# Seven-product blocks in all four feed-forward stages, woven side work in the down projections, some low parts of weights by accumulating DMA

## The chip, the cores and the metric

The kernel runs on one core of a Trainium2 chip. The metric is the device time of one execution in microseconds, as the median of several runs.

## The reference, cut to what matters

The program is two network blocks after each other on a sequence of 512 tokens with 1024 features. The first has two layers, each a feed-forward stage, a token mixing (three kinds of attention) and another feed-forward stage. The second is a state-space and a gated linear recurrence, merged and projected, with a gated side input. The four feed-forward stages are what the change touches most:

```
def swiglu(h, w_gate, w_up, w_down):
    return (jax.nn.silu(h @ w_gate) * (h @ w_up)) @ w_down

for l in range(DEPTH):                                   # 2
    x = x + 0.5 * swiglu(rmsnorm(x, ffn1_norm[l]), ...)  # 1024 -> 2816 -> 1024
    x = x + token_mixing(rmsnorm(x, mix_norm[l]), ...)
    x = x + 0.5 * swiglu(rmsnorm(x, ffn2_norm[l]), ...)
x = rmsnorm(x, final_norm)
x = second_block(x, ...)
```

## The kernel before, in words

Activations lie with features on the partitions: eight tiles `xt[m]` of 128 x 512. Every product of two float32 matrices is made of three matmuls on rounded operands (`mm3`, lines 171 to 173): high part by high part, high part of the weights by the low part of the activations, low part of the weights by the high part of the activations. So each weight tile is split after it is loaded: `wload` (line 155) loads up to 1024 columns into one of three `raw` buffers on SP's queue, ScalarE copies each piece of 512 columns to the rounded high part `whi` (line 164), VectorE subtracts to get the low part `wlo` (line 165). There are four buffers for each of the two. `split` (line 175) does the same for activations and for the blocks' weight sums.

Four feed-forward stages run in the order 0 to 3, with a mixing after stages 0 and 2. Stages 0 and 3 go through `ffn` (line 227): in two halves, 11 row groups of gate and up products of 8 x 3 matmuls with 512 columns each, then the down projection over all eight output tiles. A `hook` is a generator with side work, one step of which is issued before each row group: `positions` (line 420) builds the attention biases for stage 0, `prepare` (line 1001) the tables and operands of the second block's recurrence for stage 3.

Stages 1 and 2 go through `ffn_blocks` (line 319). The first four row groups are plain; meanwhile `blocks` (line 330) combines halves of the activations. The other 18 row groups go in pairs through `gate_up` (line 275): each pair of row groups (`j` 0 for gate, 1 for up) is a 2 x 2 block product made with seven products in place of eight, by sums of weight blocks (`s1` to `s4`, made on VectorE at lines 284 to 287) and of activation blocks; each product is 4 x 3 matmuls with 256 columns. One such pass of seven products takes two raw buffers, and 14 pieces for the split weights, which `piece` (line 268) hands out in turn from the buffers of `whi` and `wlo` and twelve more. The activation tiles `xh`, `xl` are overwritten with the combined activations by 16 splits when the plain rows are done. After row groups 8, 16 and 22 a down projection of that group's rows follows and adds to `xt`.

`block2` (line 1158) is the second block. In its front half four generators (`s5`, `lru`, `merge_gates`, `first_norm`) are stepped in a fixed order of fractions; their projections load weights by `wload` as well, and POOL does some elementwise products (lines 1231, 1309, 1326).

All waits come from the tile framework. It also sets the order of the instructions in each engine's queue by a schedule that it makes at build time, with the program's order as priority; the engines then run their queues in order.

Of the kernel before, what the change touches and what calls it, by code (L numbers as in the profile page):

```python
# [17 lines left out]
P = 128  # L18
# [34 lines left out]
BLOCKS = (1, 2)  # L53
# [46 lines left out]
def body(tc, A, out, tap, upto=99):  # L100
# [7 lines left out]
    with ctx:  # L108
# [45 lines left out]

        def wload(src, n):
# [3 lines left out]
            for i in range(0, n, WP):  # L159
# [5 lines left out]
                weng[0].tensor_tensor(lo[:, :w], r, hi[:, :w].bitcast(F32), op=ALU.subtract)  # L165
# [61 lines left out]
        def ffn(i, nxt, pre, hook=None):  # L227
            with tc.tile_pool(name=f"fp{i}", bufs=1, reuse_waits="tile") as fp:
                for hf in range(2):
                    hh, hl = [], []  # L230
                    for f in range(NH):
                        ff = hf * NH + f
                        if hook is not None and ff >= 1:
                            if ff == 1:
                                work = hook(fp)
                            next(work, None)
                        gp = psum("pg")
                        up = psum("pu")
                        for j, o in ((0, gp), (1, up)):
                            wh, wl = ahead if i == ff == j == 0 else wload(A[f"gu{i}"][ff, :, j, :], KD * P)  # L240
                            for k in range(KD):
                                c = slice(k * P, (k + 1) * P)
                                mm3(o, wh[:, c], wl[:, c], xh[KORD[k]], xl[KORD[k]], k == 0, k == KD - 1)
                            if ff == 0:
                                next(pre)
                        t = tmp("t")
                        u = tmp("u")
                        V.tensor_tensor(t, gp, rstd, op=ALU.mult)
                        act(t, t, AF.Silu)
                        V.tensor_tensor(u, up, rstd, op=ALU.mult)  # L250
                        V.tensor_tensor(u, u, t, op=ALU.mult)
                        a = fp.tile([P, S], F32R, tag="h", name="hh", bufs=2 * NH)
                        b = fp.tile([P, S], F32R, tag="h", name="hl", bufs=2 * NH)
                        split(a, b, u)
                        hh.append(a)
                        hl.append(b)
                    for m in range(KD):
                        o = psum("pd")
                        for k0, k1 in ((0, 6), (6, NH)):
                            wh, wl = wload(A[f"dn{i}"][m][:, (hf * NH + k0) * P:(hf * NH + k1) * P], (k1 - k0) * P)  # L260
                            for k in range(k0, k1):
                                c = slice((k - k0) * P, (k - k0 + 1) * P)
                                mm3(o, wh[:, c], wl[:, c], hh[k], hl[k], k == 0, k == NH - 1)
                        V.scalar_tensor_tensor(out=xt[m], in0=o, scalar=0.5, in1=xt[m], op0=ALU.mult, op1=ALU.add)
                        if hf == 1 and nxt is not None:
                            nxt.tile(m)

# [7 lines left out]
        def gate_up(p, j, xk, fp, turn):  # L275
# [43 lines left out]
        def ffn_blocks(i, nxt, pre):  # L319
            with tc.tile_pool(name=f"fp{i}", bufs=1, reuse_waits="tile") as fp:  # L320
# [32 lines left out]
                for g, (f0, f1) in enumerate(FGRP):  # L353
# [8 lines left out]
                    for p in range(f0 // 2, f1 // 2):  # L362
                        if p < NCLS:
                            for f in (2 * p, 2 * p + 1):
                                t, u = None, None
                                for j in range(2):
# [22 lines left out]
                                    if f > 0 and len(ts) < KD:  # L389
                                        blocks(len(ts) // 2)  # L390
# [1236 lines left out]
```

## Time and profile before

| | us |
|---|---|
| median of 3 runs | 2675.55 (2673.48 to 2675.76) |
| the profiled execution | 2671.1 |
| its span, first to last instruction | 2669.3 |
| TensorE busy | 2563.2 (96%) |
| VectorE busy | 1852.2 (69%) |
| ScalarE busy | 1290.5 (48%) |
| GpSimd busy | 108.9 (4%) |

PE is TensorE's matmuls, PEld its weight loads, DVE VectorE, ACT ScalarE, POOL GpSimd, SP the engine that issues the loads. Busy time is a union of an engine's instructions; matmuls overlap, so the mean duration of one is longer than the distance from one start to the next. A stage's limit is read from a table of stretches: how much of the stretch each engine is busy, and who waits for whom in it.

### The profile page before, as it was taken

Reading aid. Unit: us, or ns where it says so; the run is one execution under the profiler, and the core shown is the slowest. Engines: PE = TensorE matmul, PEld = TensorE weight load, DVE = VectorE, ACT = ScalarE, POOL = GpSimd, SP = SyncE. Lnnn points to the kernel's source line nnn. Section 1 sums busy time; section 2 is a strip of 40 time slices with the busy share of each in tenths; the row PEclk is TensorE's granted clock in tenths of the full one; section 3 lists DMA queues with packets and bytes.
Section 4 is the critical chain, followed back from the end, with each engine's and each line's share of the span. In section 5 each row is a group of like instructions: output and inputs, shape, how many; then the busy total and the mean of one; then the engine's idle time right before and its main releaser. Section 6 shows DMA issues by size and latency. Waiting matters only on the chain.

```text
span 2669.3 us, 36064 instructions
## 1 busy us (share of the span) xinstructions
PE 2563.2 (96%) x13140; PEld 2132.9 (80%) x13140; DVE 1852.2 (69%) x3533; ACT 1290.5 (48%) x2382; POOL 108.9 (4%) x113
## 2 busy tenths in 40 slices
PE   8999999999999999899999999999999978889998
PEld 6888888777789998889888877788888767668885
DVE  8634457888777586867676888766464699994435
ACT  5423346656445454535355666543343454563342
POOL 0000000000000000000000000000000013210001
PEclk9999999999999999999999999999999989989998
DMA  7432245763233332232335575233342444323332
GB/s 236 135 102 95 89 148 176 223 200 91 96 103 103 95 105 93 79 104 95 111 107 186 172 237 146 93 134 124 124 152 84 154 143 140 123 75 123 102 107 91
DMA packets 124354, 340.12 MB, mean 127 GB/s; under 512 B 17296, under 2 KB 25488, under 8 KB 123664
## 3 DMA queue, kind: packets, MB, share of 16 engines
q1 hardware_dynamic: 124176, 337.82, 40.1%
q8 instruction: 103, 1.69, 0.3%
q14 instruction: 75, 0.61, 0.1%
HBM read 279.56 MB, written 51.90 MB: 124 GB/s over the span
## 4 chain that ended last, share of the span: by engine, by line
PE 79%; DVE 14%; DMA 3%; ACT 2%; issue 2%; POOL 0%; POOLq 0%; SPq 0%; DVEq 0%; ACTq 0%
PE pd L172 6%; PE pd L171 6%; PE pd L173 6%; PE pg L171 4%; PE pg L172 4%; PE pg L173 4%; PE pu L171 3%; PE pu L172 3%; PE pu L173 3%; PE s L554 2%; PE sy L171 2%; DMA raw<-in_gu 2%; PE sy L173 2%; PE sy L172 2%; PE tp L583 1%
## 5 line engine op out<-in xcount | busy, mean ns | idle before, releaser
L164 ACT ACTIVATE whi<-raw 128x512 fp32r<-128x512 f32 (+1 forms) x738 | 431.8, 590 | 782.0 <-PE pd L172 237.9
L165 DVE TENSOR_TENSOR wlo<-raw,whi 128x512 fp32r<-128x512 f32 (+1 forms) x738 | 475.1, 649 | 366.9 <-ACT whi L164 319.4
L172 PE MATMUL pd<-hl,whi 128*128 128x512 f32 x704 | 278.1, 395 | 0.0
L173 PE MATMUL pd<-hh,wlo 128*128 128x512 f32 x704 | 278.1, 395 | 0.0
L171 PE MATMUL pd<-hh,whi 128*128 128x512 f32 x704 | 278.0, 395 | 0.0
L171 PE MATMUL pg<-xh,whi 128*128 128x512 f32 x480 | 192.4, 401 | 7.7 <-ACT xh L211 7.7
L172 PE MATMUL pg<-xl,whi 128*128 128x512 f32 x480 | 191.0, 398 | 0.3 <-DVE xl L212 0.3
L173 PE MATMUL pg<-xh,wlo 128*128 128x512 f32 x480 | 190.6, 397 | 0.0
L173 PEld LDWEIGHTS pd<-hh,wlo 128*128 128x128 f32 x704 | 132.0, 187 | 32.2
L171 PEld LDWEIGHTS pd<-hh,whi 128*128 128x128 f32 x704 | 132.0, 187 | 32.1
L172 PEld LDWEIGHTS pd<-hl,whi 128*128 128x128 f32 x704 | 132.0, 187 | 32.0
L171 PE MATMUL pu<-xh,whi 128*128 128x512 f32 x384 | 152.3, 397 | 0.0
L172 PE MATMUL pu<-xl,whi 128*128 128x512 f32 x384 | 151.6, 395 | 0.0
L173 PE MATMUL pu<-xh,wlo 128*128 128x512 f32 x384 | 151.3, 394 | 0.0
L171 PE MATMUL sy<-xh,wsp 128*128 128x256 f32 x432 | 123.0, 285 | 5.4 <-ACT c L304 4.2
L176 ACT ACTIVATE wsp<-fs 128x512 fp32r<-128x512 f32 x144 | 88.1, 627 | 70.3 <-DVE fs L284 43.1
L172 PE MATMUL sy<-xl,wsp 128*128 128x256 f32 x432 | 121.2, 280 | 0.0
L173 PE MATMUL sy<-xh,wsp 128*128 128x256 f32 x432 | 121.1, 280 | 0.0
L171 PEld LDWEIGHTS pg<-xh,whi 128*128 128x128 f32 x480 | 90.9, 189 | 29.9 <-ACT xh L211 8.7
L172 PEld LDWEIGHTS pg<-xl,whi 128*128 128x128 f32 x480 | 90.7, 189 | 23.4 <-DVE xl L212 2.2
L173 PEld LDWEIGHTS pg<-xh,wlo 128*128 128x128 f32 x480 | 90.8, 189 | 22.3
L177 DVE TENSOR_TENSOR wsp<-fs,wsp 128x512 fp32r<-128x512 f32 x144 | 92.2, 685 | 6.0 <-ACT wsp L176 5.6
(629 smaller groups left out, 6471.4 us busy)
## 6 DMA issues: line engine op xcount, KB each, us to landing
raw<-in_gu SPq DMA_DIRECT2D x176, 512.0 KB, 3.6
raw<-in_w SPq DMA_DIRECT2D x44, 512.0 KB, 3.7
raw<-in_dn SPq DMA_DIRECT2D x48, 384.0 KB, 3.2
b<-bias SPq DMA_DIRECT2D x64, 256.0 KB, 4.0
raw<-in_dn SPq DMA_DIRECT2D x32, 512.0 KB, 3.6
raw<-in_wf SPq DMA_DIRECT2D x28, 512.0 KB, 4.4
raw<-in_dn SPq DMA_DIRECT2D x32, 320.0 KB, 2.9
raw<-in_wo SPq DMA_DIRECT2D x16, 512.0 KB, 3.7
```

The source lines that it names most:

```text
L164: act(hi[:, :w], r, AF.Copy)
L165: weng[0].tensor_tensor(lo[:, :w], r, hi[:, :w].bitcast(F32), op=ALU.subtract)
L171: nc.tensor.matmul(o, wh, ah, start=first, stop=False, skip_group_check=more)
L172: nc.tensor.matmul(o, wh, al, start=False, stop=False, skip_group_check=more)
L173: nc.tensor.matmul(o, wl, ah, start=False, stop=last, skip_group_check=more)
L176: act(dst_h, src, AF.Copy)
L177: eng.tensor_tensor(dst_l, src, dst_h.bitcast(F32), op=ALU.subtract)
L554: nc.tensor.matmul(sps, a[:, c], b, start=i == 0, stop=i == len(passes) - 1)
L583: nc.tensor.transpose(tp[:, k * P:(k + 1) * P], e[:, k * P:(k + 1) * P], ident)
```

## The change

All four stages go through one `ffn`, which is the old `ffn_blocks` with a hook. The hook's generator is stepped in the down projections, by a count for each of the three groups: 4, 4, 1 for `positions`, 7, 8, 4 for `prepare`. Its tiles come from a pool that is open during one down projection, and the blocks' extra pieces and sums from a pool that is open during one group of row pairs, so that both use the same memory. The passes' weights are made by `blocks_of`, apart from their products; for the first pass this stands ahead of the 16 activation splits.

`lowpart` makes a low part in one of two ways: by VectorE as before, or by a ScalarE copy with scale -1 into the low tile and a DMA from POOL's queue that adds the raw weights to it. The second way is used for `a12` and `a22` of every pass, for plain row groups 1 to 3 of every stage, and for all weights in the front half of `block2`.

```diff
-BLOCKS = (1, 2)
+LDMA = ("a12", "a22")
...
+        def lowpart(lo, r, hi, by_dma):
+            if by_dma:
+                act(lo, r, AF.Copy, scale=-1.0)
+                G.dma_start(out=lo.bitcast(F32), in_=r, accum_op=ALU.add)
+            else:
+                V.tensor_tensor(lo, r, hi.bitcast(F32), op=ALU.subtract)
...
-                weng[0].tensor_tensor(lo[:, :w], r, hi[:, :w].bitcast(F32), op=ALU.subtract)
+                lowpart(lo[:, :w], r, hi[:, :w], weng[0] is None)
...
-        def gate_up(p, j, xk, fp, turn):
+        def blocks_of(p, j, xk, fp, turn):
...
-                ws[n] = piece(fp, turn), piece(fp, turn)
-                split(*ws[n], w)
+                ws[n] = h, lo = piece(fp, turn), piece(fp, turn)
+                act(h, w, AF.Copy)
+                lowpart(lo, w, h, n in LDMA)
+            return ws
+
+        def gate_up(ws, xk):
...
-        def ffn_blocks(i, nxt, pre):
+        class Late:
+
+
+            def tile(self, *a, **k):
+                return self.pool.tile(*a, **k)
+
+        def ffn(i, nxt, pre, gain, hook=None, steps=(0, 0, 0)):
...
+                late = Late()
+                work = hook(late) if hook else iter(())
...
+                        weng[0] = V if f == 0 else None
+                        wh, wl = ahead if i == f == j == 0 else wload(W[f, :, j, :], KD * P)
+                        weng[0] = V
...
+                for f in range(2 * NCLS):
+                    rows(f)
                 for g, (f0, f1) in enumerate(FGRP):
...
+                    with tc.tile_pool(name=f"fw{i}{g}", bufs=1, reuse_waits="tile") as fw:
+                        turn = [0]
+                        for p in range(max(f0 // 2, NCLS), f1 // 2):
+                            ws = blocks_of(p, 0, xk, fw, turn)
+                            if p == NCLS:
                                 for m, t in enumerate(ts):
                                     split(xh[m], xl[m], t)
...
+                            row_pair(lambda: gate_up(ws, xk), lambda: gate_up(blocks_of(p, 1, xk, fw, turn), xk))
                     n = f1 - f0
...
+                    with tc.tile_pool(name=f"fq{i}{g}", bufs=1, reuse_waits="tile") as late.pool:
+                        done = 0
+                        for m in range(KD):
+                            o = psum("pd")
+                            wh, wl = wload(A[f"dn{i}"][m][:, f0 * P:f1 * P], n * P)
...
+                            while done < steps[g] * (m + 1) / KD:
+                                next(work, None)
+                                done += 1
                         if f1 == NF:
+                            for _ in work:
+                                pass
...
         def block2(pre):
+            weng[0] = None
...
+                weng[0] = V
                 with tc.tile_pool(name="bd", bufs=1, reuse_waits="tile") as bd:
...
-                    if 2 * l in BLOCKS:
-                        ffn_blocks(2 * l, nrm, (cur.done(), f"ffn1_norm{l}"))
-                    else:
-                        ffn(2 * l, nrm, cur.done(), positions if l == 0 else None)
+                    ffn(2 * l, nrm, cur.done(), f"ffn1_norm{l}", positions if l == 0 else None, (4, 4, 1))
...
+                    ffn(2 * l + 1, nrm, cur.done(), f"ffn2_norm{l}", prepare if l + 1 == DEPTH else None, (7, 8, 4))
```

In `positions` the tiles of the row positions are loaded and converted three times (`along`) in place of once, with twelve buffers in place of seven; in `prepare` there are five buffers in place of six and one table buffer in place of two, and `kk` is loaded for each quarter.

## Rows read from the trace of the kernel before

**Rows 1.** The page, part 1: busy us, share of the span, instructions.

```profile
PE 2563.2 (96%) x13140; PEld 2132.9 (80%) x13140; DVE 1852.2 (69%) x3533; ACT 1290.5 (48%) x2382; POOL 108.9 (4%) x113
```

**Rows 2.** Stretches: start:end length, busy us (count) per engine, clock, DMA.

```profile
core 0: us, PE busy (x) PEld busy (x) DVE busy (x) ACT busy (x) POOL busy (x), PEclk, DMA share, GB/s
...
684.50:1042.80 358.30, 351.85 (x2245) 317.77 (x2244) 262.39 (x458) 175.84 (x332) 1.01 (x1) 0.99 0.30 97
1042.80:1409.00 366.20, 354.65 (x2246) 318.44 (x2245) 262.42 (x458) 173.74 (x331) 1.01 (x1) 0.99 0.32 101
...
1710.60:2092.20 381.60, 381.60 (x1694) 308.98 (x1693) 230.72 (x543) 158.38 (x278) 5.25 (x13) 1.00 0.37 121
2092.20:2410.00 317.80, 275.88 (x1184) 215.78 (x1183) 284.64 (x467) 173.95 (x259) 64.20 (x66) 0.92 0.39 127
```

**Rows 3.** Stretches inside the stages, columns as in rows 2.

```profile
199.00:322.00 123.00, 123.00 (x529) 98.95 (x528) 56.42 (x87) 40.64 (x66) 0.00 (x0) 1.00 0.28 89
730.50:779.00 48.50, 42.31 (x338) 41.71 (x337) 42.06 (x74) 26.46 (x55) 0.00 (x0) 0.93 0.31 105
779.00:824.00 45.00, 45.00 (x196) 36.20 (x195) 22.82 (x36) 13.66 (x23) 0.00 (x0) 1.00 0.27 87
824.00:904.00 80.00, 79.77 (x671) 79.53 (x670) 65.63 (x120) 45.88 (x93) 0.00 (x0) 1.00 0.31 100
1089.00:1139.60 50.60, 43.07 (x338) 41.76 (x337) 42.15 (x74) 26.19 (x55) 0.00 (x0) 0.93 0.32 99
1184.40:1268.60 84.20, 81.27 (x674) 80.11 (x673) 66.01 (x120) 45.68 (x94) 0.00 (x0) 1.00 0.30 96
1710.60:1840.50 129.90, 129.90 (x590) 105.68 (x589) 98.13 (x284) 58.15 (x99) 4.05 (x7) 1.00 0.38 130
1902.10:2030.60 128.50, 128.50 (x578) 104.33 (x577) 75.19 (x145) 54.24 (x93) 1.20 (x6) 1.00 0.38 130
```

**Rows 4.** TensorE's waits, 730 to 779 us: who waited, us in total, times, longest.

```profile
PE sy L173 <- DVE wsp L177: 5.4, 1, 5.4
```

**Rows 5.** Chain that ended last, 1184 to 1270 us: start, us, what.

```profile
1211.86 4.23 DMA raw<-in_gu
...
1221.85 4.29 DMA raw<-in_gu
```

**Rows 6.** Timeline around 1216 us: start, us, instruction, idle time before and its releaser.

```profile
1216.18 0.69 DVE L284 TENSOR_TENSOR fs<-raw 128x512 f32<-128x512 f32 x1 [2.48 <-DMA raw<-in_gu]
...
1216.97 0.63 ACT L176 ACTIVATE wsp<-fs 128x512 fp32r<-128x512 f32 x1 [1.95 <-DVE fs L284]
1217.51 0.36 ACT L304 ACTIVATE c<-sy 128x256 f32<-128x256 f32 x1
```

**Rows 7.** TensorE's waits, 1184.4 to 1375 us, columns as in rows 4.

```profile
PE sy L171 <- ACT c L304: 3.7, 6, 1.4
```

**Rows 8.** Groups of instructions, 824 to 904 us: shapes, count, busy us, mean ns, idle.

```profile
L177 DVE TENSOR_TENSOR wsp<-raw,wsp 128x512 fp32r<-128x512 f32 x21 | 14.1, 685 | 1.5 <-ACT wsp L176 1.3
...
L176 ACT ACTIVATE wsp<-raw 128x512 fp32r<-128x512 f32 x21 | 13.0, 631 | 7.4 <-PE sy L172 5.6 <-ACT c L308 1.0 <-ACT wsp L176 0.5
```

**Rows 9.** DMA queues (packets, MB, share) and issues (KB each, us to landing).

```profile
q1 hardware_dynamic: 124176, 337.82, 40.1%
...
qka<-sta SPq DMA_DIRECT2D x16, 256.0 KB, 5.1
...
gd<-g SPq DMA_DIRECT2D x8, 256.0 KB, 2.0
```

**Rows 10.** Groups and waits of the last block's front half, 2130 to 2410 us.

```profile
L165 DVE TENSOR_TENSOR wlo<-raw,whi 128x512 fp32r<-128x512 f32 (+1 forms) x74 | 54.1, 747 | 4.9 <-ACT whi L164 4.7
...
PE yp L172 <- DVE hs L177: 10.7, 7, 2.3
PE yp L171 <- ACT hs L176: 10.7, 4, 5.7
...
L1326 POOL TENSOR_TENSOR g<-g,e 128x512 f32<-128x512 f32 x10 | 14.9, 1493 | 57.1 <-ACT e L1325 57.1
L1309 POOL TENSOR_TENSOR c<-c,ig 128x512 f32<-128x512 f32 x10 | 14.8, 1483 | 54.7 <-ACT ig L1307 54.6
```

More of the change, by code (lines that the diff above doesn't have):

```diff
@@ L225, in done @@
                 yield col
[L227 to L266, printed above, removed]
         def piece(fp, turn):
@@ new lines, in ffn, with finish, rows @@
+                hh, hl = [], []
+                def finish(u):
+                    a, b = htile("hh"), htile("hl")
+                    split(a, b, u)
+                    hh.append(a)
+                    hl.append(b)
+                def rows(f):
+                    o = [None, None]
+                    for j in range(2):
+                        o[j] = psum("pg")
+                        weng[0] = V if f == 0 else None
+                        wh, wl = ahead if i == f == j == 0 else wload(W[f, :, j, :], KD * P)
+                        weng[0] = V
+                        for k in range(KD):
+                            c = slice(k * P, (k + 1) * P)
+                            mm3(o[j], wh[:, c], wl[:, c], xh[KORD[k]], xl[KORD[k]], k == 0, k == KD - 1)
+                        if f == 0:
+                            next(pre)
+                        elif len(ts) < KD:
+                            blocks(len(ts) // 2)
+                    t, u = tmp("t"), tmp("u")
+                    V.tensor_tensor(t, o[0], rstd, op=ALU.mult)
+                    act(t, t, AF.Silu)
+                    V.tensor_tensor(u, o[1], rstd, op=ALU.mult)
+                    V.tensor_tensor(u, u, t, op=ALU.mult)
+                    finish(u)
@@ L437, in positions, with along @@
                 V.tensor_copy(lo, it)
+            def along():
+                pi, pt, rh, rl = tmp("pi", I32), tmp("pt", I32), tmp("rh"), tmp("rl")
+                dma(pi, A["posr"])
+                parts(pi, pt, rh, rl)
+                return rh, rl
+            parts(ci, ct, ch, cl)
             for q in range(4):
+                if q % 2 == 0:
+                    rh, rl = along()
                 d = tmp("d")
@@ L1002, in tmp @@
             def tmp(name):
[L1003 removed]
+                return fp.tile([P, S], F32, tag="pz", name=name, bufs=5)
             def softplus():
@@ L1087, in prepare @@
             for ct in range(4):
+                kk = fp.tile([P, 256], F32, tag="kk", name="kk")
+                dma(kk, A["kk"])
                 g4 = slice(4 * ct, 4 * ct + 4)
@@ L1530, in body @@
                     weng[0] = V
-                    if 2 * l + 1 in BLOCKS:
-                        ffn_blocks(2 * l + 1, nrm, (cur.done(), f"ffn2_norm{l}"))
-                    else:
-                        ffn(2 * l + 1, nrm, cur.done(), prepare if l + 1 == DEPTH else None)
+                    ffn(2 * l + 1, nrm, cur.done(), f"ffn2_norm{l}", prepare if l + 1 == DEPTH else None, (7, 8, 4))
                     for m in range(KD):
```

92 lines of the change are left out of this document (24 added, 68 removed).

## The prediction

> **What bounds the kernel now.** I began with the busy line of the page: TensorE is busy 2563 of 2669 us [rows 1]. VectorE, at 69%, bounds only where a stage makes it late. So two things can be sold: matmul columns, and the about 106 us in which TensorE has nothing to run. The stretches of the second view show where each lies [rows 2]. The fourth feed-forward stage, written as plain products like the first, has no idle time: 381.6 us busy of 381.6. The second and the third, already in seven-product blocks, take 358.3 and 366.2 us, 6.4 and 11.5 us of it idle. The front half of the last block (2092 to 2410) is different: VectorE is busy 284.6 of 317.8 us, TensorE 275.9, at a mean granted clock of 0.92.
>
> Then the parts of a stage [rows 3]. In plain rows 529 matmuls of 512 columns start in 123.0 us, 0.2325 us each. In blocks, where a matmul has 256 columns, 671 take 80.0 us in the second stage (0.119 us each, against a half of 0.2325, 0.116) and 674 take 84.2 us in the third (0.125). The first two block pairs of both stages are the weak place: 336 matmuls should take 39.1 us and take 48.5 and 50.6. The wait there is one: 5.4 us for the low part of the first weight piece [rows 4]. It sits on VectorE behind the 16 splits of the combined activations, which can start only when the plain rows have read the old ones.
>
> Last, the chain of waits in the third stage [rows 5]: the longest pieces of it are loads of raw weights, and one follows another after 10.0 us, about one seven-product pass (84 matmuls, 9.8 us). There are three raw buffers and a pass needs two, so the second load of a pass waits for the low part of `a12` of the pass before. Then ScalarE, in order, waits for the sum `s1` with the copy that empties a PSUM bank behind it [rows 6]; TensorE waits for that copy, 3.7 us in the 14 passes of the second and third group [rows 7]. So this loop has no slack left.
>
> **The change part by part**, against the profiled execution (span 2669.3 us, 2671.1 us with what lies around it; the median of the runs shown, 2675.55, is 4.4 more, and I carry the difference over unchanged).
>
> 1. Columns. A plain stage has 22 row groups x 2 x 8 x 3 = 1056 gate and up matmuls of 512 columns. The blocks keep four rows plain (192) and run the other 18 as 9 pairs x 2 x 7 products x 4 x 3 = 1512 of 256. 864 x 0.2325 = 200.9 us go, 1512 x 0.1163 = 175.8 come: -25.1 us a stage, **-50.2 us** for two. TensorE is the bound there, so this is on the path.
>
> 2. What blocks cost beyond columns. A block stage should take 720 x 0.2325 + 175.8 = 343.2 us and about 2.6 for the norm's small matmuls, 346. The second stage is 12 us over this, the third 20. Two more such stages at their mean: **+32 us**, if nothing else changed.
>
> 3. The start of the blocks. The diff puts the weights of the first pass ahead of the 16 activation splits. The low part that waited is then ready when the rows end. The second product still needs all four even activations: the chain of splits, seven at 0.67 us in sequence (14.1 us for 21 [rows 8]) behind the first copy (0.63), takes 5.3 us, with 2.4 us of matmuls to run meanwhile. I leave 2.5 to 4.5 us a stage of the 9.4 and 11.5 that stand now; 4.5 taken, four stages: **-24 us** against item 2's level (bounds -10 to -32).
>
> 4. Accumulating DMA in the blocks. Per pass two of seven low parts leave VectorE (685 ns each [rows 8]); a copy with scale -1 on ScalarE (631 ns) and a DMA from POOL replace each (144 such transfers, 48 more in the plain rows, 74 in block2). VectorE's 65.6 of 80.0 us [rows 3] falls by some 10 us, ScalarE's 45.9 rises to 56; neither is then a bound. The price is delay: the trace has no DMA from POOL and none that adds, all program traffic is of one hardware queue [rows 9]. The nearest are plain transfers of 256 KB: 2.0 us to landing for a store of `g`, 5.1 for `qka`. As the transfer also reads its destination, the far end is twice the longer, 10.2; below 2.0 excluded by the same size. I take 5.1, the one with the most traffic beside it. The weights themselves have room: twenty pieces hold ten products, so the place of `a12` is free when three products of the pass before are done (4.2 us into it, 1.4 each), and the part is used at 16.8, 11.3 us after its two copies. In the plain rows each buffer comes free at 2.8 us into a load of 5.6 and is used at 11.7: 7.7 us after two copies. So 5.1 is hidden, 10.2 is not. The raw buffer is the tight spot: 4.2 + 1.3 (two copies) + 5.1 + 4.3 (load) = 14.9 us, so the load lands 5.1 us into the next pass and not 0.1. `s1` is wanted at 11.2 us, so this fits too, provided that ScalarE is given the next `a12` ahead of `s1`. The order in the queues is made by a scheduler at build time and doesn't follow the program: ScalarE's bank copies stand between the splits [rows 6]. I take it that it fits: **-10 us** for four stages (from an excess of 2.6 and 8.5 us beyond item 3 to about 3 each; bounds -20 to +216, see the rivals).
>
> The Trainium skill, "DMA: Bandwidth & Descriptors", Anatomy of one DMA, fits a transfer issued from GpSimd with 2.0 us plus bytes over 436 GB/s: an estimate of 2.6 us for 256 KB by that page. No run here shows it; by it the raw load would land 2.5 us into the next pass, and the sum would not change. The same page's rules for kernel authors say that an accumulating transfer reads its destination and writes it later, which speaks against its fit for a plain copy holding here.
>
> 5. Woven work. `positions` and `prepare` leave the plain rows, where they were free, for the down projections. These have room: VectorE is busy 22.8 of 45.0 us [rows 3]. `positions` is about 50 operations of at most 0.69 us, 35 us of VectorE over three such stretches: hidden, at nothing (5 us if the first block's sums wait for its buffers, which now share memory with the hook's). `prepare`: 98.1 and 75.2 us in its two stretches of rows against 56.4 per 123 without it, so about 55 us, of which seven steps of nineteen, with the long first part, some 32, meet 22 us of room in the first down projection. Its stores (four of 1664 KB) pass SP's queue between the weight loads, which run up to three ahead. And the first block after it can't start its sums until the hook's last tile is let go. **+5 us** (0 to +20). Its matmuls (about 110, the surplus of x1694 over 1584 [rows 2]) stay on TensorE.
>
> 6. The last block's front half. All 74 low parts leave VectorE: 54.1 us [rows 10] of a stretch in which it is 284.6 of 317.8 us busy [rows 2]. TensorE's two largest waits there are for `hs`, which VectorE makes and feeds, 10.7 us each; all its idle time is 41.9 us. But POOL works in order, and its 20 products wait for ScalarE (57.1 and 54.6 us); a DMA queued behind one of these waits with it. Gain bounded by about three quarters of the idle time, -30; loss by 20 times the 1.5 us that such a product takes, +30. I take **-10 us**.
>
> Sum: -50.2 + 32 - 24 - 10 + 5 - 10 = -57 us: 2614 by the profile, **2618 us** on the scale of the median. The forecast's own range is 2588 to 2645.
>
> **The rivals.**
>
> R0, only the columns arrive (17%): the scheduler puts the activation splits ahead as now, the raw loop stays as tight as it is, and block2 gains nothing. -50.2 + 32 + 5 = -13: 2662 us. For it: blocks have left this stall in both stages where they run. Against it: the diff reverses the very order that causes it.
>
> R1, POOL becomes late in block2 (9%): its products and 74 DMA issues share one queue, and each of 20 waits exposes some 2 us to TensorE: +40 instead of -10, 2668 us. For it: the waits of POOL for ScalarE. Against it: two loads are always prepared ahead.
>
> R2, slower: the raw-buffer loop (17%). If ScalarE's queue has `s1` ahead of the next `a12`, the late load delays the copy that frees the PSUM bank. Now the load lands 0.1 us into the pass and TensorE loses up to 1.4 us [rows 7]; at 5.1 us it would lose about 3 per pass, 72 passes in four stages, +216 instead of -10: 2844 us. Each microsecond of it is 72 us; from 0.7 us a pass on (47 us without item 4's gain, over 72) it eats the whole gain. With 2 us it is 2772. For it: the chain shows this loop as the binding one in the third stage. Against it: in the second stage the same passes take 0.119 us a matmul and not 0.125 [rows 3], so the loop can run without loss.
>
> **How the numbers follow.** Forecast 57%, R0 17, R1 9, R2 17. 0.2% (5.4 us) is about what a measurement of this kernel can tell from no change. Faster by more than it: all of the forecast, 15 of R0, 5 of R1: 0.77. Within it: 0.05. Slower: R2 with the rest of R1: 0.18. The range from 2588 to 2690 leaves some 5% below and 15% above, most of R2.
>
> **What the profile would show.** First and fourth stage at some 358 to 370 us with matmuls of 256 columns at 0.117 to 0.12 us; the wait at the first block for an activation's low part and 2 to 4 us long (item 3); loads of raw weights off the chain in the third stage, landing 4 to 6 us into a pass (item 4); VectorE below 80% from 2100 us on and fewer waits for `hs` (item 6). Accumulating transfers that land later than 8 us after their copy, or waits of TensorE for `sy` banks of over 1 us in every pass, would make the prediction wrong.

## The result and the profile after

| | before | after |
|---|---|---|
| median | 2674.52 us | 2751.41 us (2745.44 to 2753.88) |
| ratio | | 1.0288 [1.0267, 1.0309] |
| span of the profiled execution | 2669.3 us | 2743.7 us |

The change makes the kernel 2.9% slower. The forecast was 2618 us with a range to 2690; the time is above it, near rival R2 with 2 us a pass, 2772. One of the four executions of e12 below ran at a mean granted clock of 0.852, where the other three had 0.983 to 0.985, took 4% longer, and is left out of its median.

The page of after, part 1 (busy us, share, instructions) and part 4 (the chain that ended last, by line):

```profile
PE 2558.6 (93%) x14436; PEld 2184.1 (80%) x14436; DVE 1883.3 (69%) x3645; ACT 1501.0 (55%) x2877; POOL 333.9 (12%) x379
...
DMA raw<-in_gu 6%; PE pd L180 5%; PE pd L178 5%; PE pd L179 5%; DMA wsp<-raw 4%; PE s L549 2%; PE pg L178 2%; PE pg L180 2%; PE pg L179 2%; PE sy L178 2%; PE sy L179 1%; DMA wlo<-raw 1%; PE sy L180 1%; PE tp L578 1%; PE po L180 1%
```

Against [rows 1] TensorE is busy for less of the span (93%, before 96%). Loads of raw weights and the new accumulating transfers, `wsp<-raw`, stand in the chain with 6 and 4% of the span.

Where the time went: the table of stretches of after, the four feed-forward stages, the last block's front half and, after the dots, the eight passes between two down projections of the second stage. Columns: stretch, its length, busy us and instructions of PE, PEld, DVE, ACT, POOL, then granted clock, DMA share, GB/s. The second fence has the first stage before, which [rows 2] leave out.

```profile
0.00:392.10 392.10, 364.82 (x2245) 322.75 (x2246) 281.02 (x617) 212.98 (x416) 43.31 (x55) 0.99 0.59 163
691.40:1069.60 378.20, 358.65 (x2246) 319.41 (x2245) 232.05 (x410) 196.04 (x380) 42.41 (x49) 1.00 0.49 126
1069.60:1451.80 382.20, 361.61 (x2246) 322.07 (x2245) 232.39 (x411) 194.89 (x379) 42.35 (x49) 0.99 0.50 129
1752.40:2174.00 421.60, 384.74 (x2342) 340.79 (x2341) 295.25 (x676) 228.45 (x441) 46.87 (x58) 0.96 0.51 139
2174.00:2490.00 316.00, 274.52 (x1211) 214.96 (x1210) 247.57 (x402) 212.60 (x340) 123.25 (x144) 0.95 0.75 191
...
833.00:923.00 90.00, 82.89 (x671) 80.23 (x671) 59.19 (x108) 52.66 (x109) 12.04 (x14) 1.00 0.54 136
```

```profile
0.00:383.60 383.60, 375.67 (x1597) 300.33 (x1598) 212.84 (x471) 148.30 (x256) 1.83 (x7) 1.00 0.41 132
```

The loss is in the stages. The second and third, which were blocks before as well, went from 358.3 and 366.2 [rows 2] to 378.2 and 382.2 us; the fourth from 381.6 to 421.6; the first, 383.6 long before, to 392.1. The four together grew by 84 us, and what follows the fourth shrank by 7 (from 577.1 to 569.7). The last row of the first fence is the stretch of [rows 3] in the second stage: the same 671 matmuls that started in 80.0 us take 90.0, 0.134 us each and not 0.119, while VectorE is less busy than before (59.2, was 65.6) and ScalarE far from full. So no engine bounds a pass; something is waited for in turn.

What that is: the page's rows of two groups (busy, mean ns | idle time before them and what ended it), its DMA issues (count, KB, median us to landing), then SP's waits in 833 to 923 us (total, times, longest) and two of TensorE's waits over the whole span:

```profile
L158 POOL DMA_DIRECT2D wsp<-raw x144 | 124.0, 870 | 1058.7 <-ACT wsp L157 590.8
L250 DVE TENSOR_TENSOR fs<-raw 128x512 f32<-128x512 f32 x72 | 49.8, 692 | 145.7 <-DMA raw<-in_gu 145.5
...
raw<-in_gu SPq DMA_DIRECT2D x176, 512.0 KB, 3.9
wsp<-raw POOLq DMA_DIRECT2D x144, 256.0 KB, 3.6
wlo<-raw POOLq DMA_DIRECT2D x112, 256.0 KB, 4.3
```

```profile
SPq L246 <- DMA wsp<-raw: 69.1, 11, 13.5
...
PE sz L180 <- DVE wsp L160: 20.9, 22, 1.5
...
PE sx L180 <- DMA wsp<-raw: 9.3, 10, 2.2
```

VectorE stands idle for 2.0 us before the first sum `s1` of a pass on average (145.5 us in 72), because the raw load has not landed. In the kernel before, the same row reads 26.1 us in 36 passes, 0.7 us each:

```profile
L284 DVE TENSOR_TENSOR fs<-raw 128x512 f32<-128x512 f32 x36 | 24.8, 690 | 26.2 <-DMA raw<-in_gu 26.1
```

And the load has not landed because it could not start: SP, which issues it, waits for accumulating transfers to let go of a raw buffer. TensorE feels it through what stands behind the late sum, weight parts and the copies and additions that empty PSUM banks: its waits in the blocks' products (`sx`, `sy`, `sz`) come to 91 us in nine rows, against 23 in e1 below. Only 9.3 us of them are waits for a transfer itself, for the low part of `a12` (`sx`).

One turn of that loop, from the timeline (start, us, engine, line, operation, idle before it):

```profile
867.71 0.62 ACT L257 ACTIVATE wsp<-raw 128x512 fp32r<-128x512 f32 x1
...
873.28 0.69 DVE L250 TENSOR_TENSOR fs<-raw 128x512 f32<-128x512 f32 x1 [4.22 <-DMA raw<-in_gu]
...
874.07 0.63 ACT L257 ACTIVATE wsp<-fs 128x512 fp32r<-128x512 f32 x1 [3.28 <-DVE fs L250]
...
877.87 1.14 ACT L257 ACTIVATE wsp<-raw 128x512 fp32r<-128x512 f32 x2
...
879.43 0.62 ACT L157 ACTIVATE wsp<-raw 128x512 fp32r<-128x512 f32 x1
...
880.34 0.86 POOL L158 DMA_DIRECT2D wsp<-raw  x1 [11.38 <-ACT wsp L157]
...
888.13 0.69 DVE L250 TENSOR_TENSOR fs<-raw 128x512 f32<-128x512 f32 x1 [2.25 <-DMA raw<-in_gu]
```

The first load of this pass is there at 867.7, when ScalarE copies `a11` from it. `a12` lies in the same buffer, but its copies stand behind those of the four sums, and the first of these waits 3.3 us for `s1`, which waits for the pass's second load. So `a12` is copied at 877.9 and negated at 879.4, 11.7 us after `a11`; POOL issues the transfer at 880.3; the load into the buffer that it frees stands in the chain from 883.75 to 888.1, and only then can VectorE start the next sum, 14.9 us after this one. A pass of matmuls takes 9.8 us. In two of the seven passes that begin in this stretch `a12` got ahead of the sums, in five it did not.

### The profile page after: what moved, and what is told of

It reads as the page before. It is cut to its first block, busy times and chain, and to the rows that moved or that the text cites. A ratio compares the mean times of both kernels' runs of the same rounds, so it can differ in the third digit from the quotient of the medians.

```text
span 2743.7 us, 40155 instructions
## 1 busy us (share of the span) xinstructions
PE 2558.6 (93%) x14436; PEld 2184.1 (80%) x14436; DVE 1883.3 (69%) x3645; ACT 1501.0 (55%) x2877; POOL 333.9 (12%) x379
## 4 chain that ended last, share of the span: by engine, by line
PE 54%; DMA 14%; issue 13%; DVE 12%; ACT 4%; POOL 2%; POOLq 0%; SPq 0%; DVEq 0%; ACTq 0%
DMA raw<-in_gu 6%; PE pd L180 5%; PE pd L178 5%; PE pd L179 5%; DMA wsp<-raw 4%; PE s L549 2%; PE pg L178 2%; PE pg L180 2%; PE pg L179 2%; PE sy L178 2%; PE sy L179 1%; DMA wlo<-raw 1%; PE sy L180 1%; PE tp L578 1%; PE po L180 1%
## 5 line engine op out<-in xcount | busy, mean ns | idle before, releaser
L171 ACT ACTIVATE whi<-raw 128x512 fp32r<-128x512 f32 (+2 forms) x562 | 334.2, 601 | 571.4 <-PE pd L179 205.6
L160 DVE TENSOR_TENSOR wlo<-raw,whi 128x512 fp32r<-128x512 f32 (+2 forms) x440 | 283.4, 650 | 191.1 <-ACT whi L171 186.4
L178 PE MATMUL sy<-xh,wsp 128*128 128x256 f32 x864 | 253.4, 293 | 46.5 <-ACT c L274 15.1
L158 POOL DMA_DIRECT2D wsp<-raw x144 | 124.0, 870 | 1058.7 <-ACT wsp L157 590.8
L180 PE MATMUL sy<-xh,wsp 128*128 128x256 f32 x864 | 246.7, 286 | 0.1
L179 PE MATMUL sy<-xl,wsp 128*128 128x256 f32 x864 | 246.1, 285 | 0.2
L178 PEld LDWEIGHTS sy<-xh,wsp 128*128 128x128 f32 x864 | 166.3, 192 | 60.0 <-ACT c L274 19.3
L160 DVE TENSOR_TENSOR wsp<-fs,wsp 128x512 fp32r<-128x512 f32 x288 | 188.5, 682 | 8.8 <-ACT wsp L257 8.5
L257 ACT ACTIVATE wsp<-raw 128x512 fp32r<-128x512 f32 x216 | 133.0, 623 | 81.2 <-DMA raw<-in_gu 55.6
L158 POOL DMA_DIRECT2D wlo<-raw x122 | 106.9, 905 | 535.0 <-ACT wlo L157 500.0
L180 PEld LDWEIGHTS sy<-xh,wsp 128*128 128x128 f32 x864 | 166.9, 193 | 0.8 <-DVE wsp L160 0.7
L179 PEld LDWEIGHTS sy<-xl,wsp 128*128 128x128 f32 x864 | 166.7, 193 | 0.6 <-DVE xl L184 0.6
L250 DVE TENSOR_TENSOR fs<-raw 128x512 f32<-128x512 f32 x72 | 49.8, 692 | 145.7 <-DMA raw<-in_gu 145.5
L391 DVE SCALAR_TENSOR_TENSOR xt<-pd,xt 128x512 f32<-128x512 f32 x96 | 66.1, 689 | 65.6 <-PE pd L180 65.2
```

Of the source, the lines that this page charges most:

```text
L158: G.dma_start(out=lo.bitcast(F32), in_=r, accum_op=ALU.add)
L160: V.tensor_tensor(lo, r, hi.bitcast(F32), op=ALU.subtract)
L171: act(hi[:, :w], r, AF.Copy)
L178: nc.tensor.matmul(o, wh, ah, start=first, stop=False, skip_group_check=more)
L179: nc.tensor.matmul(o, wh, al, start=False, stop=False, skip_group_check=more)
L180: nc.tensor.matmul(o, wl, ah, start=False, stop=last, skip_group_check=more)
```

## The experiments

Each difference is to the kernel before, measured beside it on the same chip; after itself is +76.9 us. Theory A is this loop (rival R2): raw load, sums, ScalarE's splits in order, the low part of `a12`, release of the buffer, next load. In its narrow form it is the transfer's reading of the raw buffer alone that costs; the whole loop is called A' where the two are told apart. Its rivals: ScalarE's 144 added copies cost the time themselves; the woven work does; the transfers in the last block or in the plain rows do; the transfers land too late for the products that use them.

**e1: the blocks' low parts all by VectorE again.**

```diff
-LDMA = ("a12", "a22")
+LDMA = ()
```

> The change, but with all seven low parts of a pass made by VectorE again (no accumulating transfer in the blocks; those of the plain rows and of block2 stay). Theory A, the raw-buffer loop: the transfer holds the raw buffer of a11 and a12 some 3 us longer, so the next pass's load is late. Without it the passes go from 0.135 us a matmul back to the 0.119 to 0.125 of the kernel before: some 14 to 18 us in each of four stages, 2680 to 2695 us. Theory B, ScalarE: its extra copies and the order of its queue cost the time; also back, as the copies go as well. Theory C, the blocks cost what they cost and the loss is from the woven work and the pools that are opened for each group: no more than 10 us, 2740 us.

2643.47 us, −23.8 (0.9905 [0.9885, 0.9925]). The transfers in the blocks alone cost 101 us, more than the 14 to 18 us a stage that was expected, and all the rest of the change together is a gain. Rows of e1's table of stretches: the second and the fourth stage and the eight passes of the second; then its row of `s1`:

```profile
671.50:1026.80 355.30, 352.13 (x2245) 316.65 (x2244) 255.24 (x446) 180.05 (x344) 11.40 (x13) 1.00 0.35 107
...
1686.80:2072.10 385.30, 371.70 (x2342) 332.79 (x2341) 315.35 (x713) 210.84 (x405) 15.59 (x21) 0.98 0.40 128
...
807.00:888.00 81.00, 80.55 (x673) 79.91 (x672) 67.81 (x121) 46.33 (x94) 0.00 (x0) 1.00 0.30 99
...
L250 DVE TENSOR_TENSOR fs<-raw 128x512 f32<-128x512 f32 x72 | 49.8, 692 | 61.2 <-DMA raw<-in_gu 60.9
```

The wait for the load falls to 0.8 us a pass (0.7 before the change), and 673 matmuls start in 81.0 us. VectorE at 84% does not bound them.

**e5: the copies stay on ScalarE, the addition goes to VectorE.**

```diff
-                lowpart(lo, w, h, n in LDMA)
+                if n in LDMA:
+                    act(lo, w, AF.Copy, scale=-1.0)
+                    V.tensor_tensor(lo, w, lo.bitcast(F32), op=ALU.add)
+                else:
+                    lowpart(lo, w, h, False)
```

> The change, but the low parts of a12 and a22 are made by the change's ScalarE copy with scale -1 and then an addition on VectorE in place of the transfer. ScalarE's queue has the same copies as the change, VectorE the load of the kernel before, and nothing holds a buffer for long. Theory A (the time a transfer holds a buffer that a later step of the same loop needs): as with all low parts by VectorE, 2640 to 2655 us. Theory B (ScalarE's extra copies, in order with the bank copies): as the change, 2730 to 2755 us.

2650.33 us, −20.0 (0.9929 [0.9914, 0.9944]): within 4 us of e1. ScalarE's added copies are not the cause; the transfer is.

**e3: a fourth raw buffer for the blocks.** Every second pass gets one of its two buffers from the group's pool.

```diff
-                r = wp.tile([P, WMAX], F32, tag="raw", name="raw", bufs=NRAW)
+                if turn[0] // 14 % 2 == 1 and f % 2 == 1:
+                    r = fp.tile([P, WMAX], F32, tag="raw4", name="raw", bufs=1)
+                else:
+                    r = wp.tile([P, WMAX], F32, tag="raw", name="raw", bufs=NRAW)
```

> The change, with a fourth raw buffer in the blocks (the second load of every other pass goes to a buffer of its own), so that a load waits for the pass before the last and not for the last one. Transfers, copies and their order of work stay. Theory A: the loop is open, 0.117 to 0.120 us a matmul, 20 us and more gained in each stage, 2640 to 2680 us. Theory B (ScalarE's copies or the transfers' delay on the weights themselves): no gain, 2740 to 2755 us. Theory C: the same, 2745 us.

2666.62 us, −0.6 (1.0001 [0.9988, 1.0014]). The transfers and copies stay, and one more buffer takes back 77.5 of the 101 us. This is the run that shows theory A. Its table of stretches for the second stage's eight passes, and its row of `s1`:

```profile
819.00:903.60 84.60, 81.97 (x675) 80.49 (x674) 57.49 (x104) 53.92 (x108) 12.05 (x14) 1.00 0.56 141
...
L253 DVE TENSOR_TENSOR fs<-raw 128x512 f32<-128x512 f32 x72 | 49.8, 692 | 104.1 <-DMA raw<-in_gu 103.9
```

The loop is eased and not open: 0.125 us a matmul where 0.117 to 0.120 was expected, and the load is still late by 1.4 us a pass. f1 below asks for the rest.

**e2: the transfers for sums instead of raw parts.** `s4` and `s3` lie in sum buffers, so their transfers hold no raw buffer.

```diff
-LDMA = ("a12", "a22")
+LDMA = ("s4", "s3")
```

> The change, but the two low parts of a pass that go by accumulating transfer are those of the sums s3 and s4 and not of a12 and a22: the same number of transfers and of ScalarE copies, but the transfer reads a sum's buffer, not a raw one. Theory A (raw-buffer loop): the raw buffer is free as early as in the kernel before and VectorE is relieved all the same, so 0.118 to 0.125 us a matmul, 2665 to 2690 us. Theory B (ScalarE's extra copies, or the transfers as such): no gain, 2740 to 2755 us. Theory C: 2745 us.

2734.55 us, +67.3 (1.0252 [1.0234, 1.0271]): hardly better than after, and far from theory A's range. So the narrow form of A, that the transfer is dear because it reads a raw buffer, falls. Two runs ask what is left of A.

**e9: e2 with eight sum buffers in place of four.**

```diff
-            s1, s2, s3, s4 = (fp.tile([P, WP], F32, tag="fs", name="fs", bufs=4) for _ in range(4))
+            s1, s2, s3, s4 = (fp.tile([P, WP], F32, tag="fs", name="fs", bufs=8) for _ in range(4))
```

> As the run in which the transfers make the low parts of s3 and s4 (2734.6 us), with eight buffers for the sums in place of four. Theory A in its wider form: there the transfers held the sums' buffers and not the raw ones, and the loop was as tight; with eight it opens: 2640 to 2665 us. Theory B (ScalarE's copies, or transfers that land too late for the products): 2720 to 2740 us as before.

2720.88 us, +50.5 (1.0189 [1.017, 1.0209]): the sum buffers give 17 us, no more, and the time lies in theory B's range. e9's row of `s1`, its raw loads, two of TensorE's waits over the whole span, and ScalarE's timeline in one pass:

```profile
L250 DVE TENSOR_TENSOR fs<-raw 128x512 f32<-128x512 f32 x72 | 49.8, 692 | 97.4 <-DMA raw<-in_gu 97.4
...
raw<-in_gu SPq DMA_DIRECT2D x176, 512.0 KB, 4.8
...
PE sz L180 <- DMA wsp<-fs: 12.0, 9, 3.0
PE sy L180 <- DMA wsp<-fs: 12.0, 9, 3.7
```

```profile
853.99 0.62 ACT L157 ACTIVATE wsp<-fs 128x512 fp32r<-128x512 f32 x1
854.51 0.62 ACT L257 ACTIVATE wsp<-fs 128x512 fp32r<-128x512 f32 x1
855.03 0.62 ACT L157 ACTIVATE wsp<-fs 128x512 fp32r<-128x512 f32 x1
855.55 1.67 ACT L257 ACTIVATE wsp<-raw 128x512 fp32r<-128x512 f32 x3
```

The load is still late by 1.35 us a pass. The two negated copies for `s4` and `s3` (line 157, 0.52 us from start to start) now stand ahead of the copies of the raw parts, 1.0 us later for `a12`, and a raw load takes 4.8 us where e1's page has 4.0. Both lengthen the same loop, which [rows 5] showed to have no slack. The rival has a share: TensorE waits 24.0 us for the transfers of `s4` and `s3` themselves. And the wait at `s1` alone does not measure a loss, for e3 has as much of it and is 51 us faster.

**e11: e9 with e3's fourth raw buffer.**

> The low parts of s3 and s4 by transfer, eight buffers for the sums (2720.9 us), and now a fourth raw buffer. Theory A', the loop of the raw buffers in all its legs: load, sums, ScalarE's splits in order, low part of a12, next load. There the two ScalarE copies stood ahead of a12 (1.1 us) and the loads landed later beside the transfers (4.8 us against 4.0), so the loop was as long as with a12 by transfer though no transfer held a raw buffer. With a fourth buffer it opens: 2645 to 2665 us. Rival: the transfers of s3 and s4 come too late for their products, whatever the buffers: 2705 to 2725 us.

2634.28 us, −39.0 (0.986 [0.9845, 0.9874]), 89.5 us better than e9 by one buffer. The second stage's eight passes are back at 675 matmuls in 80.6 us, and the wait is e1's:

```profile
804.00:884.60 80.60, 80.50 (x675) 80.23 (x674) 58.41 (x104) 54.48 (x109) 12.91 (x15) 1.00 0.59 143
...
L253 DVE TENSOR_TENSOR fs<-raw 128x512 f32<-128x512 f32 x72 | 49.5, 688 | 62.2 <-DMA raw<-in_gu 61.9
```

This is 15 us better than e1, too. TensorE's waits for the transfers themselves fall with it, from 24.0 to 6.0 us. So A' holds for both kinds of delay of the last reader of a raw buffer, a transfer from it (e3) and two copies ahead of its split with slower loads (e9).

**e13: `a12` and `a22` ahead of the sums**, the order that item 4 of the prediction took for granted.

```diff
-            for n, w in (("a11", a11), ("s1", s1), ("s2", s2), ("s4", s4), ("s3", s3), ("a12", a12), ("a22", a22)):
+            for n, w in (("a11", a11), ("a12", a12), ("a22", a22), ("s1", s1), ("s2", s2), ("s4", s4), ("s3", s3)):
```

> The change, with a12 and a22 split directly after a11 and ahead of the four sums; transfers, buffers and copies are the same in number. Theory A': the low part of a12 then no longer waits for the sums of the late load, the raw buffer is released some 4 us earlier in the pass, and the loop opens although the transfer holds it: 2645 to 2685 us. Rival: the delay of the transfer as such decides, or the pieces' turn binds in its place: 2735 to 2760 us.

2685.03 us, +11.7 (1.0049 [1.0032, 1.0066]): 65 us better than after. But the passes did not come back to 0.120, as A' had them:

```profile
820.00:909.00 89.00, 82.70 (x673) 81.55 (x672) 59.73 (x107) 52.41 (x106) 11.19 (x13) 0.98 0.57 143
...
PE sy L178 <- DVE c L282: 24.4, 26, 2.4
```

673 matmuls in 89.0 us, 0.132 each. The gain came elsewhere: the first two pairs of the second stage take 44.0 us in place of 50.4, and the eight passes of the fourth 0.130 us a matmul in place of 0.151. The load is still late by 1.4 us a pass (99.2 us in 72), and TensorE's largest wait over the span (second line) is for an addition that empties a PSUM bank, as in f1 below. The rival of the expectation, that the pieces' fixed turn binds instead, is not borne out: in this stretch ScalarE waits 3.2 us in six times for TensorE to read a piece's old holder in `sy`, and 3.7 us in six in e1, whose passes run freely. So the order is worth 65 us, and a mere change of it was not the cure that item 4 had assumed.

**f1: after with five raw buffers**, two from the group's pool in every second pass.

```diff
-                if turn[0] // 14 % 2 == 1 and f % 2 == 1:
-                    r = fp.tile([P, WMAX], F32, tag="raw4", name="raw", bufs=1)
+                if turn[0] // 14 % 2 == 1:
+                    r = fp.tile([P, WMAX], F32, tag="raw4", name="raw", bufs=2)
```

(This edit is on e3.)

> The change, a12 and a22 by transfer, with five raw buffers: every other pass has two of its own. Theory A': the loop of the raw buffers, which with four still closed over two passes for the second load alone, is wide open: 0.119 to 0.121 us a matmul, 2635 to 2648 us. Rival: the transfers of the last two parts land too late for their products or hold ScalarE's order: as with four buffers, 2660 to 2670 us.

2671.95 us, +0.7 (1.0009 [0.9994, 1.0024]): the same as e3, and not the 2635 to 2648 of A'. Some 24 us of the transfers' price are left that more raw buffers do not remove. TensorE's largest wait over the span, in e3 and in f1, and what lies ahead of it on VectorE in one pass of f1:

```profile
PE sy L178 <- DVE c L285: 24.5, 21, 2.3
...
PE sy L178 <- DVE c L285: 33.1, 21, 5.4
```

```profile
855.61 0.69 DVE L253 TENSOR_TENSOR fs<-raw 128x512 f32<-128x512 f32 x1 [2.89 <-DMA raw<-in_gu]
...
858.97 0.41 DVE L285 TENSOR_TENSOR c<-sy,c 128x256 f32<-128x256 f32 x1
```

The addition that empties a PSUM bank (line 285) stands in VectorE's queue behind a sum that waits 2.9 us for its load. TensorE waits for this addition 24.5 us in e3, 2.0 in e1 and 1.8 in e11, which is about the size of what is left. Why the loads still come late with five buffers (1.3 us a pass), and why the schedule puts the addition behind the sum with transfers from raw parts and not with e11's, was not settled.

**e6: `prepare` spread over three stages**, on e1. Its steps go 3 and 4 into the second stage, 4 and 4 into the third, 4 into the fourth, and no rest is drained at the end of the second and third.

```diff
-                        if f1 == NF:
+                        if f1 == NF and i in (0, 3):
...
-                    ffn(2 * l, nrm, cur.done(), f"ffn1_norm{l}", positions if l == 0 else None, (4, 4, 1))
+                    ffn(2 * l, nrm, cur.done(), f"ffn1_norm{l}", pos if l == 0 else prep, ((4, 4, 1), (4, 4, 0))[l])
...
-                    ffn(2 * l + 1, nrm, cur.done(), f"ffn2_norm{l}", prepare if l + 1 == DEPTH else None, (7, 8, 4))
+                    ffn(2 * l + 1, nrm, cur.done(), f"ffn2_norm{l}", prep, ((3, 4, 0), (4, 0, 0))[l])
```

> All low parts of the blocks by VectorE (2643.5 us so far), and the steps of prepare spread over the down projections of three stages, one quarter in each and the long first part alone, where the change puts seven, eight and four steps into those of the fourth. Theory: the fourth stage is 29 us longer than the second and third in that kernel, 10 of it the hook's matmuls; the other 19 are VectorE's overload in its down projections and the wait of the next sums for the hook's tiles. Spread, most of these 19 go: 2622 to 2632 us. Rival: they are the hook's cost wherever it stands, or are paid in three stages: 2640 to 2650 us.

2615.94 us, −54.4 (0.9799 [0.9783, 0.9816]): 30.6 us better than e1. The eight passes of the fourth stage in e1 and, in the second fence, in e6, and e6's fourth stage:

```profile
1824.00:1910.30 86.30, 82.24 (x674) 80.40 (x673) 73.75 (x132) 49.27 (x101) 1.05 (x2) 1.00 0.32 105
1910.20:1960.40 50.20, 50.20 (x243) 41.30 (x242) 45.52 (x155) 23.16 (x41) 1.11 (x2) 1.00 0.51 177
```

```profile
1833.80:1914.30 80.50, 80.48 (x674) 80.08 (x673) 67.81 (x121) 46.59 (x95) 0.00 (x0) 1.00 0.30 100
...
1696.20:2052.90 356.70, 354.50 (x2270) 319.42 (x2269) 271.49 (x515) 193.32 (x368) 14.15 (x18) 1.00 0.38 115
```

In e1 the hook doesn't stay in the down projection: 11 more VectorE instructions than in e6 stand in the passes behind it, which take 86.3 us and not 80.5, and in the next down projection (second row) VectorE is busy 45.5 of 50.2 us. Whether the passes wait for VectorE or for the memory that they share with the hook was not separated.

**e10: the 16 activation splits ahead of the first pass's weights**, as in the kernel before; on e1.

```diff
-                            ws = blocks_of(p, 0, xk, fw, turn)
                             if p == NCLS:
...
                                     split(xh[m], xl[m], t)
+                            ws = blocks_of(p, 0, xk, fw, turn)
```

> All low parts of the blocks by VectorE (2643.5 us), and the 16 activation splits ahead of the first pass's weights again, as in the kernel before. If that order was the cause of the 5.4 us wait at the first block (item 3 of the prediction), the wait comes back in four stages: +16 to +24 us, 2660 to 2668. If the schedule set the order anyway: 2643 us.

2652.19 us, −18.2 (0.9931 [0.9911, 0.995]). The order is worth 5.6 us in four stages, 1.4 a stage, less than the 16 to 24 expected, and the intervals of e1 and e10 overlap. Nor does the wait of 5.4 us [rows 4] come back: the longest of TensorE in the blocks' products is 2.1 us, and the longest for a weight's low part 1.7.

**e4 and e12: the last block's low parts by VectorE**, in after and in e6 (`weng[0] = None` left out at the head of `block2`).

> The change, but all low parts in the front half of block2 by VectorE as before. The stretch after the fourth stage takes 569.7 us with the change and 577.1 before. If that gain is the relief of VectorE (item 6 of the prediction), it is lost: 2755 to 2762 us. If POOL's queue costs time there (rival R1) and the gain comes from elsewhere: 2735 to 2750 us.

> All low parts of the blocks by VectorE and prepare spread (2615.9 us), and the low parts of block2's front half by VectorE too. The transfers there are worth what this loses: item 6 of the prediction says 10 us (2626), the run on the whole change 14 (2630); rival R1 would have it faster, 2600 to 2612 us.

e4: 2765.31 us, +98.1 (1.0367 [1.0344, 1.0391]), 21 us worse than after. e12: 2630.3 us, −43.0 (0.9845 [0.9828, 0.9861]), 11.5 worse than e6. The transfers are a gain there; R1 is false.

**f2: the plain rows' low parts by VectorE**, on e6 (`weng[0] = V` for all four rows).

> All low parts of the blocks by VectorE, prepare spread (2615.9 us), and the low parts of the plain rows by VectorE as well. The prediction costed the rows' transfers at nothing (7.7 us of room against some 4.5 to landing): 2612 to 2620 us. Rival: they hold raw buffers there too, or relieve VectorE where it makes the combined activations: up to 10 us to either side, 2606 or 2626 us.

2624.29 us, −47.0 (0.9833 [0.9816, 0.9851]): 7.4 us worse than e6 and above the 2612 to 2620 expected, so the transfers in the plain rows gain as well; the intervals adjoin.

**e8: e6 with e3's fourth raw buffer.**

> All low parts of the blocks by VectorE, prepare spread over three stages (2615.9 us), and a fourth raw buffer. The passes there take 0.119 to 0.122 us a matmul where 0.1163 is the columns' share. Theory A': the rest is the same loop: 5 to 15 us, 2600 to 2611 us. Rival: VectorE, at over 80% in the passes, keeps the rest: 2612 to 2620 us.

2609.08 us, −64.2 (0.9762 [0.9746, 0.9778]). Without any transfer in the blocks the buffer is worth 9.8 us; with them it was worth 77.5 (e3). Where the 9.8 us lie is not shown: in the run that was profiled, the slowest of the four (2615.2 us), the passes are no faster than in e6.

**f3: e8 with e9's transfers of `s4` and `s3` and eight sum buffers.**

> Prepare spread, a fourth raw buffer, s3 and s4 by transfer with eight buffers for the sums. If relief of VectorE is worth what it seems (2634.3 against 2643.5 with all parts by VectorE, there with a fourth buffer too): 2600 to 2607 us. If the fourth buffer alone gave that (2609.1 with the spread): 2607 to 2612 us.

2602.17 us, −69.1 (0.9745 [0.9726, 0.9763]): the best version, ahead of both kernels. Its table of stretches, second and fourth stage:

```profile
666.00:1022.80 356.80, 354.53 (x2269) 319.21 (x2268) 250.59 (x476) 206.70 (x394) 43.43 (x51) 1.00 0.54 142
...
1681.50:2037.50 356.00, 354.06 (x2270) 319.22 (x2269) 251.81 (x479) 212.82 (x404) 45.26 (x54) 1.00 0.54 141
```

TensorE idles some 2 us in each. VectorE is busy some 20 us less than in e6 (250.6 against 270.7, 251.8 against 271.5), and that brought 4.9 us against e8, with intervals that overlap. Little was left to gain: in the blocks' products TensorE waits 9.4 us for VectorE in e8 and 3.5 in f3.

## Why the prediction was wrong

**The step that failed is item 4**, and in it one clause: "provided that ScalarE is given the next `a12` ahead of `s1` ... I take it that it fits". In five of seven passes ScalarE makes that copy behind the sums, in the one shown 11.7 us after that of `a11` (timeline of after). Nor was it this clause alone: with the copy moved ahead in the program (e13), 65 of the 101 us came back, and the load was still 1.4 us late. So the delay of the raw buffer's release, put at nothing because it fits, was on the path. The size of the transfer was not the error: it landed in 3.6 us by the median (5.1 taken). By the stages' lengths, the transfers in the blocks cost after 105.6 us over e1 (392.1 + 378.2 + 382.2 + 421.6 against 370.6 + 355.3 + 357.3 + 385.3), 1.5 us a pass in 72 passes, where −10 was forecast. R2 had place, mechanism and slope ("72 us for each microsecond a pass"); it had 17%, and its 3 us a pass were twice the 1.5 that came. The row that spoke for it was the chain of raw loads in the third stage, one after the other every 10.0 us [rows 5]: a loop without slack, to which the change added a copy, a queue and a transfer. The argument against it, that the second stage ran without loss [rows 3], shows that the loop could run before, not that it can with more in it. And the order of ScalarE's queue was said not to follow the program and was then taken as kind. The weights' own room, "5.1 is hidden", was read nearly rightly: TensorE waits for a transfer of `a12` in 10 of 72 passes, 9.3 us.

**Items 1 to 3** (columns −50, blocks' overhead +32, first pairs −24: −42) came out near that as a sum. In e1, where the blocks have no transfers, the second and third stage fell by 3 and 9 us and the first by 13 (383.6 to 370.6); in e6 the fourth fell by 25 (381.7 to 356.7). Of these −50 the transfers in the plain rows explain 7 (f2), and some 8 to 10 are 71 of the hook's small matmuls that e6 gave to the second and third stage (x2270 and x2293 against 2246; with them these two stages are 2.6 and 7.5 us longer than in e1): about −34 is left. Item 3 by itself was mis-sized: the order of the splits is worth 1.4 us a stage (e10), not 6. Its wait at the first block, for an activation's low part, is there in e1, once a stage, but shorter than forecast (4.9 us in all, the longest 2.2). The first two pairs of the second stage took 44.7 us in e1 against 48.5 [rows 3]; most of that does not come from the order. The traces point to the plain rows' transfers: three plain rows and the two pairs behind them take 82.2 us there before, 78.4 in e1 and 80.1 in e10, and 79.0 in e6 against 82.9 in f2, which differs from e6 in these transfers alone.

**Item 5** (+5, bound 20) is a term mis-sized: spreading `prepare` gave back 30.6 us, so it cost at least that. The 22 us of room per down projection [rows 3] was read rightly, but seven, eight and four steps were poured into one such stretch after the other, and what did not fit stood in the passes behind them (e6's fences). Of the 28 us between the two profiles 19 lie in the stages (1468.5 us for the four in e1, 1449.3 in e6) and 9 in the last block, which starts behind the hook's end.

**Item 6** (−10, ±30) is right: −11.5 (e12) to −21 (e4). VectorE's load in the front half fell from 284.6 of 317.8 us [rows 2] to 247.6 of 316.0, and TensorE's wait for the low part of `hs` from 10.7 us [rows 10] to 6.4. The new waits for the transfers themselves are four rows, 9.9 us in all; the largest is shown below the wait for `hs` (TensorE's waits over the whole span of after, us, times, longest):

```profile
PE yp L179 <- DVE hs L184: 6.4, 8, 1.8
...
PE plx L180 <- DMA wlo<-raw: 5.0, 4, 2.5
```

**The plain rows' transfers**, put at nothing, gain about 7 us (f2).

With item 4 at nothing and item 5 spread (e6) the kernel takes 2615.9 us; the forecast was 2618. That closeness is in part luck: item 3 was too large, and the plain rows' gain was not in the sum.

In item 4 the Trainium skill's fit ("DMA: Bandwidth & Descriptors", Anatomy of one DMA) had given an estimate of 2.6 us for these transfers. The traces differ: 3.6 us in the passes and 4.3 elsewhere, and never under 3.2 in the passes:

```profile
DMA to landing us min/median/max: 3.2/3.6/7.1
```

By either number item 4's sum would have come out as it did, because it took the delay as hidden.

## What to carry to other kernels

Before work goes from a busy engine to a DMA, follow every buffer that the DMA reads until it is free again: if the chain of waits already shows that buffer's loads end to end, the relief of an engine that does not bound the pass buys little (4.9 us, f3 against e8), and part of what is added to the loop is paid in every pass (here the turn shown grew from 10.0 to 14.9 us, and 1.5 us a pass were paid). The copy that starts such a transfer runs where its in-order queue has it, so read that order from the trace or bound the case in which it is last; a buffer more (e3, e11) was most of the cure here, a change of order (e13) gave back two thirds. Side work should be sized against the free time of each single stretch and spread over all of them (e6).

## What the runs showed of the hardware

An accumulating DMA of 256 KB within the core's memory takes POOL 0.86 us to issue (0.870 us in the mean of 144) and lands after 3.6 us in the passes by the median. Raw loads of 512 KB beside such transfers from the sums took 4.8 us by the median in e9, against 4.0 in e1 and 3.6 in the kernel before; beside transfers from raw parts they took 3.9 in after and 4.3 in e3.

TensorE's clock fell for short times in the fourth stage of after. In the last pairs, where the engine idled 3.6 of 25.6 us, behind a down projection in which it was busy 50.3 of 50.7 us at 1.00, the table of stretches reads:

```profile
1998.70:2049.40 50.70, 50.30 (x242) 40.85 (x241) 45.64 (x156) 23.10 (x41) 1.05 (x2) 1.00 0.54 190
2049.40:2075.00 25.60, 21.98 (x165) 21.05 (x164) 15.37 (x27) 14.04 (x29) 3.48 (x4) 0.93 0.48 126
```

A mean of 0.93 is a short part of the stretch at the lower of its two levels, 1.2 of 2.4 GHz. Some of the price of waiting may have come in this way: the 2342 matmuls of this stage were busy for 384.7 us in after and for 371.7 in e1, at mean clocks of 0.96 and 0.98; how much of the 13 us is clock was not separated.
